# Five expert pairs' outputs written to DRAM rows and gathered back per token, in a decoder layer with a mixture of experts

## The chip, the cores and the metric

The kernel runs on one core of one Trainium2 chip. The metric is device time in microseconds of one execution; the kernel before takes 704.09 us (median of three runs, 701.79 to 704.62). Its engines are named as in the profile: PE is TensorE, DVE is VectorE, ACT is ScalarE, POOL is GpSimd and SP is SyncE, which issues most DMAs.

## The reference

One decoder layer over 512 tokens of width 1024: two attention branches, then a mixture of 32 experts, then a norm. The change touches the mixture alone. In float32:

```python
def hierarchical_moe(h, w_rg, b_rg, w_re, b_re, w_g, w_u, w_d):
    ...
    g_sel = jnp.argmax(g_logits, axis=-1).astype(jnp.int32)
    ...
    top_vals, top_idx = lax.top_k(e_in, EXPERT_TOPK)
    weight = p_group * jax.nn.softmax(top_vals, axis=-1)
    expert_id = g_sel[:, None] * EXPERTS_PER_GROUP + top_idx.astype(jnp.int32)
    ...
    def expert_block(args):
        xb, e = args
        return (jax.nn.silu(xb @ w_g[e]) * (xb @ w_u[e])) @ w_d[e]
    ...
    out = jnp.zeros((T, D), h.dtype).at[slot_tok].add(ys * slot_w[:, None])
```

Each token chooses one of four groups and two of its eight experts. It is computed by these two, and their outputs, weighted, are added to its row. An expert has three matrices of 1 MB: gate and up (1024 x 256) and down (256 x 1024).

## The kernel before

The attention part runs to about 396 us, the output projection with the routing to about 435 us, and the experts from there to the end. The last two parts matter here.

**Routing.** For each of the four tiles of 128 tokens, DVE finds the group and the two experts (`choose_group`, `choose_experts`), PE counts the places of the tokens within their experts (`ranks`), and DVE turns these into one-hot matrices (`hot`, `AB`) with which PE finds the token of each slot and the first pair's rows. The tile `Mk` holds the two one-hot rows of a token's experts, `n` its two places. These operations are written in Python in this order, but the framework's scheduler sets the order on DVE, ACT and SP. Only PE's and POOL's order within the expert loop (and DVE's and ACT's in the last pair) is that of the code.

**Experts.** They are taken in 16 pairs; of a pair's 128 slots the first 64 belong to one expert and the rest to the other. The loop in `experts` does for pair q:

- SP issues the six loads of 1 MB for pair q+2 (`load_gu`, `load_d`). They go in turn through a ring of 20 buffers (`new_w`, `NH = 20`), and `load` lets each wait for the load two before it, so that two are under way.
- PE multiplies the gathered, transposed rows `xT` by gate (G) and up (U), 32 matmuls each (L770); ACT and DVE make `a = silu(G) * U` (L775, L776), PE transposes it (L782), ACT copies it back as `aT` (L784).
- PE makes the products `yp` with down in two halves of 512 columns (L796). `down_split` scales each by the slots' weights and splits it into a rounded part and a remainder: ACT L803, DVE L804.
- The combines put the slots' rows back to their tokens. `one_hot` makes S (slots by 512 tokens); for each half and each tile of tokens, PE multiplies S by the two parts (L816, L817) and DVE adds the result to `x2`, the residual in SBUF (L818). The eight combines of pair q are done in pair q+1, five behind U and three behind the transposes of a, where they fill PE's wait for a.
- POOL gathers the rows (`xg`) and the weights (`wg`) of pair q+2 from DRAM by an indirect DMA that skips empty slots (L729), and copies the slots' weights into a small tile `sw` (L739, L740).

In the last pair `last` adds the final norm: ACT scales the norm's gain `fin` (L882), which SP loads among the last weights, and the tiles of tokens are squared, scaled and stored.

```python
    def load(self, dst, src):
        d = self.nc.sync.dma_start(dst, src)
        if len(self.loads) >= 2:
            self.after(d, self.loads[-2])
```

Of the kernel before, what the change touches and what calls it, by code (L numbers as in the profile page):

```python
# [10 lines left out]
F32 = mybir.dt.float32  # L11
# [3 lines left out]
I32 = mybir.dt.int32  # L15
U32 = mybir.dt.uint32
AF = mybir.ActivationFunctionType
ALU = mybir.AluOpType
# [3 lines left out]
P = 128  # L22
T = 512
NT = T // P
D = 1024
# [5 lines left out]
NEG = -1e30  # L31
NE = 32
NH = 20


class Layer:
# [84 lines left out]
    def setup(self):  # L121
        nc, tc, ctx, io = self.nc, self.tc, self.ctx, self.io
        self.const = ctx.enter_context(tc.tile_pool(name="const", bufs=1, side="left"))
        self.small = ctx.enter_context(tc.tile_pool(name="small", bufs=1, side="left"))
        self.big = ctx.enter_context(tc.tile_pool(name="big", bufs=16, side="left"))
        c = self.const
        self.ident = c.tile([P, P], F32, name="ident")
        make_identity(nc, self.ident)
        self.mhalf = c.tile([P, 1], F32, name="mhalf")
        nc.gpsimd.memset(self.mhalf, -0.5)  # L130
        self.eps = c.tile([P, 1], F32, name="eps")
        c.tile([P, 24], F32, name="pad")
        nc.gpsimd.memset(self.eps, EPS * D)

    def load_consts(self):
# [472 lines left out]
    def take_weights(self):  # L608

        nc = self.nc  # L610
        ps = self.mp.tile([P, 512], F32, name="ptr", tag="m")[:, 0:NE + 1]
        for t in range(NT):
            nc.tensor.matmul(ps, self.hot[:, t], self.W[:, t], start=t == 0, stop=t == NT - 1)
        return self.slot_weights(0, ps, nc.vector)

    def clean_rows(self):

# [13 lines left out]
    def route_setup(self):  # L631
        nc, tc, io, c = self.nc, self.tc, self.io, self.const
        self.dram = dp = self.ctx.enter_context(tc.tile_pool(name="dram", bufs=1, space=bass.MemoryType.DRAM))
        self.x2d = dp.tile([T, D], F32, name="x2d")
        self.Wd = dp.tile([T, NE + 1], F32, name="Wd")
        self.wr = c.tile([P, KD, 40], F32, name="wr")
        nc.gpsimd.memset(self.wr, 0.0)
        self.load_late(self.wr[:, :, 0:4], io["w_router_group"][0].rearrange("(j p) g -> p j g", p=P))
        for g in range(4):
            self.load_late(self.wr[:, :, 8 + 8 * g:16 + 8 * g],  # L640
                              io["w_router_expert"][0, g].rearrange("(j p) e -> p j e", p=P))
        self.gpj = c.tile([P, KD], F32, name="gpj")
        self.load_late(self.gpj, io["ffn_norm"][0].rearrange("(p j) -> p j", p=P))
        self.gcol = gcol = c.tile([P, KD], F32, name="gcol")
        self.load_late(gcol, io["ffn_norm"][0].rearrange("(j p) -> p j", p=P))
        nc.vector.tensor_scalar(self.gpj, self.gpj, 32.0, None, ALU.mult)
        nc.vector.tensor_scalar(gcol, gcol, 32.0, None, ALU.mult)
        nc.vector.tensor_tensor(self.wr, self.wr, gcol.unsqueeze(2).to_broadcast([P, KD, 40]), ALU.mult)
        self.rb = c.tile([P, 40], F32, name="rb")
        nc.gpsimd.memset(self.rb, -3e38)  # L650
        self.load_late(self.rb[:, 0:4], io["b_router_group"][0:1, :].to_broadcast([P, 4]))
        self.load_late(self.rb[:, 8:40], io["b_router_expert"].rearrange("o g e -> o (g e)")
                          .to_broadcast([P, 32]))
        self.rc = c.tile([P, 33 + NT], F32, name="rc")
        self.load_late(self.rc, io["rconst"])
        self.iota32 = self.rc[:, 0:32]
        self.slot = self.rc[:, 32:33]
        self.token = self.rc[:, 33:33 + NT]
        self.tri = c.tile([P, 2, P], F16, name="tri")
        self.after(nc.gpsimd.dma_start(self.tri, io["tri"]), self.started)  # L660
        self.tm = c.tile([P, T], F16, name="tm")
        self.after(nc.gpsimd.dma_start(self.tm, io["tm"]), self.started)
        self.M = c.tile([P, NT, NE], F16, name="M")
        self.sq = c.tile([P, 2, NT], F32, name="sq")
        self.W = c.tile([P, NT, NE + 1], F32, name="W")
        self.iotaU = c.tile([P, NE], U32, name="iotaU")
        nc.vector.tensor_copy(self.iotaU, self.iota32)
# [10 lines left out]

    def load(self, dst, src):
        d = self.nc.sync.dma_start(dst, src)  # L680
        if len(self.loads) >= 2:
            self.after(d, self.loads[-2])
        self.loads.append(d)

    def load_w(self, src, how):
# [45 lines left out]
                                         bounds_check=T - 1, oob_is_err=False)  # L731
        return xg, wg

    def slot_weights(self, q, wg, eng):

        sw = self.small.tile([P, 2], F32, name="sw", tag="sw", bufs=3)
        for e in range(2):
            es = slice(64 * e, 64 * e + 64)
            eng.tensor_copy(sw[es, 0:1], wg[es, 2 * q + e:2 * q + e + 1])  # L739
        eng.tensor_copy(sw[:, 1:2], wg[:, NE:NE + 1])  # L740
        return sw[:, 0:1], sw[:, 1:2]

    def gathered_T(self, xg, xT, g):
        nc = self.nc
# [34 lines left out]
    def act_T(self, a, ps):  # L779
        nc = self.nc  # L780
        for j in range(2):
            nc.tensor.transpose(ps[:, j * P:(j + 1) * P], a[:, j * P:(j + 1) * P], self.ident)  # L782
        aT = a.rearrange("p (a b) -> p a b", b=P)
        nc.scalar.copy(aT, ps.rearrange("p (a b) -> p a b", b=P))  # L784
        return aT

    def down(self, wd, aT, sw, half):
# [24 lines left out]
    def combine(self, S, y, half, t):  # L812
# [4 lines left out]
        nc.tensor.matmul(cp, S[:, t * P:(t + 1) * P], y[1], start=False, stop=True)  # L817
        nc.vector.tensor_tensor(self.x2[t][:, hs], self.x2[t][:, hs], cp, ALU.add)  # L818

    def experts(self):  # L820
        nc, tc = self.nc, self.tc
        NP = NE // 2
# [3 lines left out]
        self.yhl = self.wp.tile([P, 2048], F32R, name="yhl", tag="whi")  # L826
        with tc.manual_schedule(engines={mybir.EngineType.PE, mybir.EngineType.Pool}):
            xT, sw, xg = {0: self.xT0}, {}, {}
            S, y, todo = None, None, []
            for q in range(NP):  # L830
                if q > 0 and q + 2 < NP:
                    wgu[q + 2], wd[q + 2] = self.load_gu(q + 2), self.load_d(q + 2)
                    if q + 2 == NP - 1:
                        self.load_final()
                if q:
                    sw[q] = self.slot_weights(q, wg, nc.gpsimd)

                def some(n):
                    for _ in range(min(n, len(todo))):
                        self.combine(S, y[todo[0][0]], *todo[0])  # L840
                        todo.pop(0)

                def between(j):
                    if q == 0 and j == 3:
                        self.tokens()
                        xg[1] = self.gather_rows(self.xi[:, 1:2], self.rows)
                    if q == 0 and j == 5:
                        sw[0] = self.take_weights()
                    if q == 0 and j == 9:
                        self.count_blocks()  # L850
                a = self.gate_up(wgu.pop(q), xT.pop(q), lambda: sw[q][1], between)
                def next_rows():
                    xT[q + 1] = self.new_xT()
                    for g in range(2):
                        self.gathered_T(xg[q + 1][0], xT[q + 1], g)
                if q == 0:
                    next_rows()
                some(5)
                aT = self.act_T(*a)
                some(3)  # L860
                if 0 < q < NP - 1:
                    next_rows()
                if q + 1 < NP:
                    wg = xg.pop(q + 1)[1]
                if q + 2 < NP:
                    xg[q + 2] = self.gather_rows(self.xi[:, q + 2:q + 3])
                S = self.one_hot(self.xf[:, q:q + 1])
                dn = wd.pop(q)
                y = [None, None]
                todo = [(h, t) for h in range(2) for t in range(NT)]  # L870
                if q == NP - 1:
                    self.last(S, dn, aT, sw[q][0])
                    break
                for h in range(2):
                    y[h] = self.down(dn, aT, sw[q][0], h)
# [159 lines left out]
class Route:  # L1035
# [60 lines left out]
    def choose_experts(self):  # L1096
# [1 line left out]
        self.v8, vi = self.tmp("v8", [8]), self.tmp("vi", [8], U32)  # L1098
        nc.vector.max(self.v8, self.es)
        nc.vector.max_index(vi, self.v8, self.es)  # L1100
        self.Mk = self.tmp("Mk", [2, NE])
        nc.vector.tensor_tensor(self.Mk, L.iotaU.unsqueeze(1).to_broadcast([P, 2, NE]),
                                vi[:, 0:2].unsqueeze(2).to_broadcast([P, 2, NE]), ALU.is_equal)
        nc.vector.tensor_tensor(L.M[:, self.t], self.Mk[:, 0], self.Mk[:, 1], ALU.add)
# [15 lines left out]

    def places(self):
        nc, L, t, N = self.nc, self.L, self.t, self.N
        n = self.tmp("n", [2])
        for c in range(2):
            nc.vector.scalar_tensor_tensor(self.es, self.Mk[:, c], 1.0, N, ALU.mult, ALU.mult, accum_out=n[:, c:c + 1])
        self.at(self.AB[:, :, 0:64], n)
# [33 lines left out]
def shape_consts():  # L1160
# [13 lines left out]
    tri[:, 0] = np.arange(P)[:, None] <= np.arange(P)[None, :]  # L1174
    tri[:, 0] += 1024.0 * np.eye(P)
    out["tri"] = tri
    rc = np.zeros((P, 33 + NT), np.float32)
    rc[:, 0:32] = np.arange(32)
    rc[:, 32] = 1025 + np.arange(P) % 64
    rc[:, 33:] = np.arange(P)[:, None] + P * np.arange(NT)[None, :] - 1024  # L1180
    out["rconst"] = rc
    out["tm"] = np.broadcast_to(np.arange(T, dtype=np.float32) - 1024, (P, T)).copy()
    return out
# [30 lines left out]
```

## Time and profile before

| what | us |
|---|---|
| median of the runs | 704.09 |
| the profiled execution | 708.18 |
| its span in the profile | 706.4 |
| PE busy | 684.0 (97%) |
| DVE busy | 399.0 (56%) |
| ACT busy | 277.3 (39%) |
| POOL busy | 70.9 (10%) |
| HBM read, written | 145.35 MB, 4.26 MB |

The profile is of one execution, whose time stands beside its span. The page's second part cuts the span into 40 slices and gives for each the busy tenths of an engine, of the granted TensorE clock and of the 16 DMA engines, and the GB/s that they moved. In a row of a group of instructions stand its line, engine and operation, output<-input, the count, then the busy time and the mean of one in ns, and the idle time before them with what ended it. SP's rows are issues of DMAs, and their times hold no transfer.

### The profile page before, as it was taken

The numbers are of one execution on the slowest core, as the hardware profiler recorded it, in microseconds if no ns is written. First come the engines' busy times: TensorE is split into PE (matmuls) and PEld (weight loads), VectorE is DVE, ScalarE is ACT, GpSimd is POOL, SyncE is SP. The second block draws the span as 40 slices with busy tenths as digits, with TensorE's granted clock in tenths as the row PEclk, the third lists the DMA queues.
The fourth block names the chain that finished last, engine by engine and source line by source line (L and its number), as shares of the span: only waits on it lengthen the run. The fifth ranks groups of instructions, "written<-read, shape, count | busy, mean of one in ns | idle before, by whom it ended". The sixth has DMA issues, their size and how long they took to land.

```text
span 706.4 us, 11377 instructions
## 1 busy us (share of the span) xinstructions
PE 684.0 (97%) x4262; PEld 526.2 (74%) x4262; DVE 399.0 (56%) x972; ACT 277.3 (39%) x623; POOL 70.9 (10%) x151
## 2 busy tenths in 40 slices
PE   8999999999999999999999999999999999999981
PEld 7998887777888888888888998665666666656641
DVE  4535957877829963433764227355554455555545
ACT  5748554555648663431332433121211211222113
POOL 1504000000000000000000013112111111121003
PEclk9999999999999999999999999999999999999997
DMA  8734431110272143213889668989999999999833
GB/s 253 137 77 84 111 120 60 60 45 17 69 170 61 44 138 119 63 57 119 269 295 370 243 220 296 401 309 365 367 344 347 364 357 379 374 354 370 319 123 121
DMA packets 73787, 148.17 MB, mean 210 GB/s; under 512 B 30939, under 2 KB 53555, under 8 KB 61953
## 3 DMA queue, kind: packets, MB, share of 16 engines
q1 hardware_dynamic: 67616, 138.69, 56.2%
q10 hardware_dynamic: 3040, 4.27, 2.3%
q0 software_dynamic: 3072, 4.46, 2.2%
q8 instruction: 35, 0.57, 0.3%
q14 instruction: 24, 0.19, 0.1%
HBM read 145.35 MB, written 4.26 MB: 212 GB/s over the span
## 4 chain that ended last, share of the span: by engine, by line
PE 90%; DMA 4%; DVE 2%; ACT 2%; issue 1%; SPq 0%; POOL 0%; POOLq 0%; ACTq 0%; DVEq 0%
PE yp L796 8%; PE G L770 7%; PE U L770 7%; PE pacc L96 5%; PE pacc L95 5%; PE pacc L94 5%; PE pacc L450 4%; PE pacc L448 4%; PE pacc L449 4%; PE cp L816 4%; PE cp L817 3%; PE ptr L421 3%; PE S L403 2%; PE O L429 2%; PE pacc L492 2%; PE pacc L494 2%
## 5 line engine op out<-in xcount | busy, mean ns | idle before, releaser
L65 DVE SCALAR_TENSOR_TENSOR wlo<-wraw,ms,whi 128x256 fp32r<-128x256 f32 (+2 forms) x134 | 68.3, 551 | 30.6 <-ACT whi L64 30.4
L64 ACT ACTIVATE whi<-wraw,ms 128x256 fp32r<-128x256 f32 (+2 forms) x134 | 67.0, 560 | 41.6 <-PE pacc L449 19.8
L818 DVE TENSOR_TENSOR x<-x,cp 128x512 f32<-128x512 f32 x128 | 78.1, 681 | 1.8 <-PE cp L817 1.8
L94 PE MATMUL pacc<-whi,hThi 128*128 128x352 f32 (+1 forms) x192 | 72.8, 379 | 0.0
L95 PE MATMUL pacc<-wlo,hThi 128*128 128x352 f32 (+1 forms) x192 | 70.2, 367 | 0.0
L96 PE MATMUL pacc<-whi,hTlo 128*128 128x352 f32 (+1 forms) x192 | 70.2, 366 | 0.0
L796 PE MATMUL yp<-w,a 128*64 128x512 f32 x256 | 60.2, 613 | 3.3 <-ACT a L784 3.3
L776 DVE SCALAR_TENSOR_TENSOR a<-U,sw,a 128x256 f32<-128x256 f32 x16 | 11.0, 687 | 84.2 <-PE U L770 78.6
L770 PE MATMUL U<-w,xT 128*64 128x256 f32 x512 | 58.5, 379 | 0.0
L770 PE MATMUL G<-w,xT 128*64 128x256 f32 x512 | 58.3, 380 | 0.0
L770 PEld LDWEIGHTS G<-w,xT 128*64 128x64 f32 x512 | 36.5, 137 | 24.6 <-issue 4.9
L816 PE MATMUL cp<-yhl,S 128*128 128x512 f32 x128 | 53.2, 416 | 0.0
L817 PE MATMUL cp<-yhl,S 128*128 128x512 f32 x128 | 50.6, 395 | 0.7 <-DVE yhl L804 0.7
L770 PEld LDWEIGHTS U<-w,xT 128*64 128x64 f32 x512 | 37.8, 137 | 17.6
L448 PE MATMUL pacc<-hThi,whi 128*128 128x512 f32 x128 | 50.4, 394 | 0.0
L450 PE MATMUL pacc<-hThi,wlo 128*128 128x512 f32 x128 | 50.3, 393 | 0.0
L449 PE MATMUL pacc<-hTlo,whi 128*128 128x512 f32 x128 | 49.9, 390 | 0.0
L804 DVE SCALAR_TENSOR_TENSOR yhl<-yp,sw,yhl 128x512 fp32r<-128x512 f32 x32 | 24.0, 751 | 34.9 <-ACT yhl L803 33.9
L416 ACT ACTIVATE E<-E,mx 128x128 f32<-128x128 f32 (+3 forms) x64 | 35.6, 558 | 20.4 <-DVE mx L413 19.6
L796 PEld LDWEIGHTS yp<-w,a 128*64 128x64 f32 x256 | 17.3, 139 | 34.3 <-issue 28.7
L803 ACT ACTIVATE yhl<-yp,sw 128x512 fp32r<-128x512 f32 x32 | 22.0, 687 | 48.3 <-PE yp L796 46.3
L94 PEld LDWEIGHTS pacc<-whi,hThi 128*128 128x128 f32 x192 | 36.4, 189 | 4.9 <-issue 1.4
(221 smaller groups left out, 1328.8 us busy)
## 6 DMA issues: line engine op xcount, KB each, us to landing
w<-in_w_exp_gate_dram SPq DMA_DIRECT2D x32, 1024.0 KB, 6.3
w<-in_w_exp_up_dram SPq DMA_DIRECT2D x32, 1024.0 KB, 6.9
w<-in_w_exp_down_dram SPq DMA_DIRECT2D x30, 1024.0 KB, 5.7
wraw<-in_w_in_dram SPq DMA_DIRECT2D x14, 1024.0 KB, 5.1
wraw<-in_w_out_dram SPq DMA_DIRECT2D x4, 1024.0 KB, 8.2
wraw<-in_w_in_dram SPq DMA_DIRECT2D x5, 704.0 KB
xs<-in_x_dram SPq DMA_DIRECT2D x4, 512.0 KB, 7.8
wraw<-in_w_o_mla_dram SPq DMA_DIRECT2D x4, 512.0 KB, 4.7
```

Source lines behind the costliest of these rows:

```text
L65: nc.vector.scalar_tensor_tensor(lo[:, k], raw[:, k], g, hi[:, k].bitcast(F32), ALU.mult, ALU.subtract)
L94: nc.tensor.matmul(ps[t][:, :ncols], act_hi[kk // 4][:, kk % 4, ts], hi[:, k], start=kk == 0, stop=False)
L95: nc.tensor.matmul(ps[t][:, :ncols], act_hi[kk // 4][:, kk % 4, ts], lo[:, k], start=False, stop=False)
L96: nc.tensor.matmul(ps[t][:, :ncols], act_lo[kk // 4][:, kk % 4, ts], hi[:, k], start=False, stop=kk == ktot - 1)
L448: nc.tensor.matmul(ps, hi[:, k, ds], self.hT[0][k // 4][:, k % 4], start=k == 0, stop=False)
L449: nc.tensor.matmul(ps, hi[:, k, ds], self.hT[1][k // 4][:, k % 4], start=False, stop=False)
L450: nc.tensor.matmul(ps, lo[:, k, ds], self.hT[0][k // 4][:, k % 4], start=False, stop=k == KD - 1)
L770: nc.tensor.matmul(GU[i][es, 0:256], xT[:, j, es], gu[e][i][:, j * 256:(j + 1) * 256], start=j == 0, stop=j == KD - 1)
L796: nc.tensor.matmul(yp[es], aT[:, j, es], wd[e][:, j * D + half * 512:j * D + half * 512 + 512], start=j == 0, stop=j == 1)
L816: nc.tensor.matmul(cp, S[:, t * P:(t + 1) * P], y[0], start=True, stop=False)
L817: nc.tensor.matmul(cp, S[:, t * P:(t + 1) * P], y[1], start=False, stop=True)
L818: nc.vector.tensor_tensor(self.x2[t][:, hs], self.x2[t][:, hs], cp, ALU.add)
```

## The change

Pairs 1, 3, 5, 7 and 9 (`VIA`) are combined in another way. Their outputs are scaled by ACT into a tile `y` of 128 slots, which POOL stores into a DRAM tensor `yd` of 5 x 128 rows (`down_out`). They have no S, no split and no combines. In pairs 10 to 13, one tile of tokens in each, POOL clears two tiles and gathers into them the rows that belong to each token's first and second expert, with an index out of bounds where that expert isn't in one of the five pairs (`take_slots`). DVE adds the two tiles to `x2` one pair later. `slot_rows` works out the row indices from `Mk` and the places, which are now kept in SBUF for all four tiles.

Further, the eight combines of the other pairs up to 8 are spread over the two pairs that follow, four in each. The slots' weights are copied by ACT behind the copy of `aT`, and the scale of silu and up is read directly from `wg`, so POOL copies nothing in the loop. `load` lets three loads be under way.

```diff
+VIA = (1, 3, 5, 7, 9)
...
     def load(self, dst, src):
         d = self.nc.sync.dma_start(dst, src)
-        if len(self.loads) >= 2:
-            self.after(d, self.loads[-2])
+        if len(self.loads) >= 3:
+            self.after(d, self.loads[-3])
...
-    def slot_weights(self, q, wg, eng):
+    def slot_weights(self, q, wg, copy):
         sw = self.small.tile([P, 2], F32, name="sw", tag="sw", bufs=3)
         for e in range(2):
             es = slice(64 * e, 64 * e + 64)
-            eng.tensor_copy(sw[es, 0:1], wg[es, 2 * q + e:2 * q + e + 1])
-        eng.tensor_copy(sw[:, 1:2], wg[:, NE:NE + 1])
-        return sw[:, 0:1], sw[:, 1:2]
+            c = copy(sw[es, 0:1], wg[es, 2 * q + e:2 * q + e + 1])
+            if q:
+                self.after(c, self.acted)
+        return sw
...
+    def slot_rows(self):
...
+        for t in range(NT):
+            for i in range(2):
+                nc.vector.scalar_tensor_tensor(junk, self.Mk[:, t, i], 1.0, self.base, ALU.mult, ALU.mult,
+                                               accum_out=rows[:, t, i:i + 1])
+        nc.vector.tensor_scalar(far, self.place, 1088.5, float(1 << 20), ALU.is_gt, ALU.mult)
+        nc.vector.tensor_tensor(rows, rows, self.place, ALU.add)
+        self.yi = c.tile([P, NT, 2], I32, name="yi")
+        nc.vector.tensor_tensor(self.yi, rows, far, ALU.add)
+
+    def down_out(self, wd, aT, sw, q):
+        nc = self.nc
+        y = self.bl.tile([P, D], F32, name="y", tag="yd", bufs=2)
+        for h in range(2):
+            nc.scalar.mul(y[:, h * 512:h * 512 + 512], self.down_products(wd, aT, h), sw)
+        i = VIA.index(q) * P
+        nc.gpsimd.dma_start(self.yd[i:i + P], y)
+
+    def take_slots(self, t, i):
+        nc = self.nc
+        y = self.bl.tile([P, D], F32, name="y", tag="yd", bufs=2)
+        nc.gpsimd.memset(y, 0.0)
+        nc.gpsimd.indirect_dma_start(out=y, out_offset=None, in_=self.yd,
+                                     in_offset=bass.IndirectOffsetOnAxis(ap=self.yi[:, t, i:i + 1], axis=0),
+                                     bounds_check=len(VIA) * P - 1, oob_is_err=False)
+        return t, y
...
-                if q:
-                    sw[q] = self.slot_weights(q, wg, nc.gpsimd)
+                r = wg[:, NE:NE + 1] if q else None
...
-                a = self.gate_up(wgu.pop(q), xT.pop(q), lambda: sw[q][1], between)
+                a = self.gate_up(wgu.pop(q), xT.pop(q), lambda: r if q else sw[0][1], between)
...
-                some(5)
+                n = min(len(todo), 4) if VIA[0] <= q <= VIA[-1] + 1 else len(todo)
+                some((n + 1) // 2 + (n > 4))
                 aT = self.act_T(*a)
-                some(3)
+                if q:
+                    sw[q] = [self.slot_weights(q, wg, nc.scalar.copy)[:, 0:1]]
+                some(n // 2 - (n > 4))
...
                     xg[q + 2] = self.gather_rows(self.xi[:, q + 2:q + 3])
+                if q == 1:
+                    self.slot_rows()
+                for t, r in taken:
+                    nc.vector.tensor_tensor(self.x2[t], self.x2[t], r, ALU.add)
+                t = q - VIA[-1] - 1
+                taken = [self.take_slots(t, i) for i in range(2)] if 0 <= t < NT else []
+                dn = wd.pop(q)
+                if q in VIA:
+                    self.down_out(dn, aT, sw[q][0], q)
+                    continue
                 S = self.one_hot(self.xf[:, q:q + 1])
```

What moves, at three places. First PE in pair 2, from U to the products with down, before (buffer numbers left out; U is the up product, cp a combine, G with `ident` the transposes of a, ptr those of the next rows):

```order
L770 MATMUL U<-w,xT 64x256 x16
...
L816 MATMUL cp<-yhl,S 128x512
L817 MATMUL cp<-yhl,S 128x512
L782 MATMUL G<-ident,a 128x128 x2
L816 MATMUL cp<-yhl,S 128x512
L817 MATMUL cp<-yhl,S 128x512
...
L747 MATMUL ptr<-ident,xg 128x128 x8
L796 MATMUL yp<-w,a 64x512 x8
```

Left out are four more pairs of cp rows ahead of the transposes and two more behind. The same place now:

```order
L778 MATMUL U<-w,xT 64x256 x16
L824 MATMUL cp<-yhl,S 128x512
L825 MATMUL cp<-yhl,S 128x512
...
L790 MATMUL G<-ident,a 128x128 x2
L824 MATMUL cp<-yhl,S 128x512
L825 MATMUL cp<-yhl,S 128x512
...
L755 MATMUL ptr<-ident,xg 128x128 x8
L804 MATMUL yp<-w,a 64x512 x8
```

One more pair of cp rows is left out on either side: of eight combines four are left, two ahead of the transposes and two behind, and so in each of pairs 1 to 10.

Second, DVE in the routing, where the second tile's experts have just been chosen (M), before (es,n gives a place, AB and hot are the one-hot matrices, f and W the routing weights):

```order
L1104 TENSOR_TENSOR M<-Mk 128x32
L1125 SCALAR_TENSOR_TENSOR es,n<-Mk,ptr 128x32 x2
L1118 SCALAR_TENSOR_TENSOR AB<-tm,n 128x2x64
L1152 SCALAR_TENSOR_TENSOR f<-f 128x1
```

and now:

```order
L1157 TENSOR_TENSOR M<-Mk 128x32
L1178 SCALAR_TENSOR_TENSOR es,place<-Mk,ptr 128x32
L836 SCALAR_TENSOR_TENSOR yjunk,yrows<-Mk,rc 128x32
L1178 SCALAR_TENSOR_TENSOR es,place<-Mk,ptr 128x32
L836 SCALAR_TENSOR_TENSOR yjunk,yrows<-Mk,rc 128x32
L1171 SCALAR_TENSOR_TENSOR AB<-tm,place 128x2x64
L1205 SCALAR_TENSOR_TENSOR f<-f 128x1
```

The operations of `slot_rows`, written in pair 1, stand among the routing, two for each tile of tokens; for tiles 1 and 2 (of 0 to 3) they stand among the place operations that AB waits for, and `hot` follows behind.

Third, ACT at the end of the loop, before (a<-G with sw is silu, COPY a<-G the copy of `aT`):

```order
L754 ACTIVATE xT<-ptr,gpj 128x128 x2
L803 ACTIVATE yhl<-yp,sw 128x512 x2
L775 ACTIVATE a<-G,sw 128x128x2
L882 ACTIVATE fin<-fin 128x1024
L784 COPY a<-G 128x256
```

and now:

```order
L811 ACTIVATE yhl<-yp,sw 128x512 x2
L783 ACTIVATE a<-G,wg 128x128x2
L792 COPY a<-G 128x256
L746 COPY sw<-wg 64x1 x2
L935 ACTIVATE fin<-fin 128x1024
```

The scale of `fin` stood ahead of the last pair's copy and stands behind it now, with the two copies of weights between.

More of the change, by code (lines that the diff above doesn't have):

```diff
@@ L131, in setup @@
         self.eps = c.tile([P, 1], F32, name="eps")
-        c.tile([P, 24], F32, name="pad")
+        c.tile([P, 16], F32, name="pad")
         nc.gpsimd.memset(self.eps, EPS * D)
@@ L613, in take_weights @@
             nc.tensor.matmul(ps, self.hot[:, t], self.W[:, t], start=t == 0, stop=t == NT - 1)
-        return self.slot_weights(0, ps, nc.vector)
+        sw = self.slot_weights(0, ps, nc.vector.tensor_copy)
+        nc.vector.tensor_copy(sw[:, 1:2], ps[:, NE:NE + 1])
+        return sw[:, 0:1], sw[:, 1:2]
     def clean_rows(self):
@@ L634, in route_setup @@
         self.x2d = dp.tile([T, D], F32, name="x2d")
+        self.yd = dp.tile([len(VIA) * P, D], F32, name="yd")
         self.Wd = dp.tile([T, NE + 1], F32, name="Wd")
@@ L653, in route_setup @@
                           .to_broadcast([P, 32]))
-        self.rc = c.tile([P, 33 + NT], F32, name="rc")
+        self.rc = c.tile([P, 33 + NT + NE], F32, name="rc")
         self.load_late(self.rc, io["rconst"])
@@ L658, in route_setup @@
         self.token = self.rc[:, 33:33 + NT]
+        self.base = self.rc[:, 33 + NT:]
         self.tri = c.tile([P, 2, P], F16, name="tri")
@@ L663, in route_setup @@
         self.M = c.tile([P, NT, NE], F16, name="M")
+        self.Mk = c.tile([P, NT, 2, NE], F32, name="Mk")
+        self.place = c.tile([P, NT, 2], F32, name="place")
         self.sq = c.tile([P, 2, NT], F32, name="sq")
@@ L783, in act_T @@
         aT = a.rearrange("p (a b) -> p a b", b=P)
-        nc.scalar.copy(aT, ps.rearrange("p (a b) -> p a b", b=P))
+        self.acted = nc.scalar.copy(aT, ps.rearrange("p (a b) -> p a b", b=P))
         return aT
@@ L818, in combine @@
         nc.vector.tensor_tensor(self.x2[t][:, hs], self.x2[t][:, hs], cp, ALU.add)
+    def slot_rows(self):
+        nc, c = self.nc, self.const
+        rows = c.tile([P, NT, 2], F32, name="yrows")
+        far = c.tile([P, NT, 2], F32, name="far")
+        junk = c.tile([P, NE], F32, name="yjunk")
+        for t in range(NT):
[21 more added lines that the diff above has]
+        return t, y
     def experts(self):
@@ L828, in experts @@
             xT, sw, xg = {0: self.xT0}, {}, {}
-            S, y, todo = None, None, []
+            S, y, todo, taken = None, None, [], []
             for q in range(NP):
@@ L866, in experts @@
                     xg[q + 2] = self.gather_rows(self.xi[:, q + 2:q + 3])
+                if q == 1:
[8 more added lines that the diff above has]
+                    continue
                 S = self.one_hot(self.xf[:, q:q + 1])
-                dn = wd.pop(q)
                 y = [None, None]
@@ L1100, in choose_experts @@
         nc.vector.max_index(vi, self.v8, self.es)
-        self.Mk = self.tmp("Mk", [2, NE])
+        self.Mk = L.Mk[:, self.t]
         nc.vector.tensor_tensor(self.Mk, L.iotaU.unsqueeze(1).to_broadcast([P, 2, NE]),
@@ L1122, in places @@
         nc, L, t, N = self.nc, self.L, self.t, self.N
-        n = self.tmp("n", [2])
+        n = L.place[:, t]
         for c in range(2):
@@ L1176, in shape_consts @@
     out["tri"] = tri
-    rc = np.zeros((P, 33 + NT), np.float32)
+    rc = np.zeros((P, 33 + NT + NE), np.float32)
     rc[:, 0:32] = np.arange(32)
     rc[:, 32] = 1025 + np.arange(P) % 64
-    rc[:, 33:] = np.arange(P)[:, None] + P * np.arange(NT)[None, :] - 1024
+    rc[:, 33 + NT:] = [64 * (2 * VIA.index(i // 2) + i % 2) - 1025 if i // 2 in VIA else 1 << 20 for i in range(NE)]
+    rc[:, 33:33 + NT] = np.arange(P)[:, None] + P * np.arange(NT)[None, :] - 1024
     out["rconst"] = rc
```

## The prediction

> **What bounds the kernel now.** I read the page's slices first, then the end of the chain of work, then SP's waits, then windows over the weight stream.
>
> ```profile
> span 706.4 us, 11377 instructions
> PE   8999999999999999999999999999999999999981
> DMA  8734431110272143213889668989999999999833
> GB/s 253 137 77 84 111 120 60 60 45 17 69 170 61 44 138 119 63 57 119 269 295 370 243 220 296 401 309 365 367 344 347 364 357 379 374 354 370 319 123 121
> ```
>
> One slice is 17.7 us. PE is busy nearly everywhere, which suggests a kernel bound by TensorE. But from slice 26 on (about 442 us) the DMA engines are at nine tenths too. Two resources are full at once, so the end of the chain has to decide.
>
> ```profile
> 636.76 3.45 PE G L770 x32
> ...
> 643.67 0.43 PE cp L816
> ...
> 646.18 0.22 PE G L782 x2
> ...
> 647.56 0.24 PE cp L817
> ...
> 648.81 3.58 PE yp L796 x16
> 652.39 3.45 PE G L770 x32
> 655.85 3.45 PE U L770 x32
> ...
> 659.81 7.13 DMA w<-in_w_exp_up_dram
> ...
> 667.00 5.80 DMA w<-in_w_exp_down_dram
> ...
> 673.42 7.27 DMA fin<-in_final_norm_dram
> ...
> 680.76 0.04 ACT fin L882
> 680.80 0.92 issue
> 681.72 0.36 ACT a L784
> ...
> 682.13 5.35 PE yp L796 x16
> ```
>
> Each row is a start, a length and what ran. A pair of experts takes PE 652.39 - 636.76 = 15.6 us, up to pair 14. Then the chain leaves PE: the last weights, issued one after another from 659.8 us, are what the last pair waits for. PE and the weight stream thus arrive together, the stream a little later. SP's waits between 450 and 676 us tell what paces the stream (total us, times, longest):
>
> ```profile
> SPq L680 <- DMA w<-in_w_exp_gate_dram: 66.3, 24, 4.2
> SPq L680 <- DMA w<-in_w_exp_up_dram: 65.9, 23, 4.5
> SPq L680 <- DMA w<-in_w_exp_down_dram: 63.8, 26, 4.0
> SPq L680 <- PE cp L817: 2.3, 9, 0.4
> SPq L680 <- PE yp L796: 1.7, 6, 0.4
> ```
>
> 196 of the 226 us SP waits for an earlier load (the limit of two under way), and about 4 us for PE to free a buffer. So the stream runs by itself and not at PE's pace. How fast it is (last three columns: granted clock, DMA share, GB/s):
>
> ```profile
> 450.00:460.00 10.00, 10.00 (x76) 7.01 (x73) 4.51 (x8) 1.09 (x2) 0.37 (x2) 1.00 1.00 397
> 566.00:567.50 1.50, 1.50 (x8) 1.24 (x7) 1.50 (x4) 0.00 (x0) 0.00 (x0) 1.00 1.00 426
> 594.50:596.20 1.70, 1.70 (x20) 1.12 (x18) 0.00 (x0) 0.43 (x1) 0.37 (x2) 1.00 0.55 145
> 450.00:650.00 200.00, 200.00 (x1360) 126.09 (x1358) 105.98 (x180) 38.76 (x76) 32.59 (x63) 1.00 0.96 359
> 450.00:676.00 226.00, 226.00 (x1544) 142.91 (x1541) 117.00 (x199) 43.94 (x85) 34.76 (x70) 1.00 0.94 351
> ```
>
> 426 GB/s while every engine has packets, 397 over the best 10 us, 351 on the average. Between lie holes such as 594.5 to 596.2 us, where half of the engines have nothing: both loads under way are nearly through, and the next has only just been issued. That is the loss which a third load can fill.
>
> **The change part by part.**
>
> *PE.* Five pairs lose their eight combines of two matmuls. In the chain above the 16 matmuls go from 643.67 to 647.80 us with 0.22 us of transposes among them: 3.9 us, 16 x 0.24. Five pairs: 18.8 us less PE work (bounds 17 to 19.5; the four combines left in each of pairs 1 to 10 keep the cover, two ahead of the transposes of a and two behind, 0.9 us each). This is worth time only as far as the weights come earlier, because PE already meets them at the end.
>
> *New traffic.* Five stores of 512 KB are 2.62 MB. The gathers fetch what five of sixteen pairs hold: on the average 5/16 of 512 x 2 slots, 320 rows of 4 KB, 1.31 MB. All of it runs on the engines that carry the weights.
>
> ```profile
> q0 software_dynamic: 2306, 3.66, 5.2%
> ```
>
> That is POOL's queue from 450 to 676 us: 3.66 MB took 5.2% of 226 us, 11.8 us or 3.2 us for a MB. By it the new 3.93 MB cost 12.6 us; by their bytes at 351 GB/s, 11.2 us; at 426, 9.2 us.
>
> *Three under way.* No run here has it, so it is bounded: from below by nothing (351 stays), from above by no hole and no slow restart at all (397 over 10 us; 426 only over 1.5 us). Taking the holes out alone gives 351 / 0.94 = 373; restarts after a hole are slow as well, and they go with it. I take **385**, the middle of 373 and 397. Before: 351 x 226 us = 79.3 MB. After: 83.2 MB at 385 = 216.1 us, **-9.9 us**. At 397: 209.6, -16.4. At 373: 223.1, -2.9. At 359: 231.8, +5.8. The break-even is 83.2 / 226 = 368 GB/s. The start hardly moves: the load issued at 450 us needs a buffer that pair 0's products free at 449 us.
>
> *The routing stage.* Eight multiplies with a sum and three small operations are written in pair 1, but the order shows them on DVE among the routing, where DVE is in the chain:
>
> ```profile
> 425.88 0.42 DVE x L497
> ...
> 428.53 0.21 DVE es L1125 x2
> ...
> 430.12 0.21 DVE hot L1118
> 430.37 1.16 PE pacc L604 x8
> ```
>
> ```profile
> L1125 DVE SCALAR_TENSOR_TENSOR es<-Mk,ptr 128x32 f32<-128x32 f32 x8 | 1.5, 183 | 0.1
> L1125 DVE DVE_READ_ACCUMULATOR es<-Mk,ptr 128x1 f32 x8 | 0.7, 81 | 0.0
> ```
>
> The like operation costs 183 + 81 ns, with some overlap 0.2 us. Four stand in DVE's way to the last but one `hot` (two for tile 1, two for tile 2); the rest falls into waits for PE, or behind it. **+0.8 us** (bounds 0 to 2.6).
>
> *The tail.* Today ACT scales `fin` ahead of the last copy of a, so the copy at 681.72 us waits for a transfer that it doesn't need. In the new order the copy stands ahead. The second half of the last products still needs the last down weights, issued at 675.7 us. **-1.2 us** (bounds -2.5 to +1: after the stop before 682.13 us the 16 products took 5.35 us, where they took 3.58 at 648.81; a PE that waits for weights earlier in the last pair can lose such 1.8 us there too).
>
> *At nothing.* The weights' copies on ACT instead of POOL (two of a column), the products' scaling (one ACT operation where there were ACT and DVE), POOL's memsets and the eight adds on DVE:
>
> ```profile
> L60 DVE TENSOR_TENSOR wlo<-wraw,whi 128x1024 fp32r<-128x1024 f32 x8 | 9.5, 1221 | 7.9 <-ACT whi L59 7.9
> L620 POOL MEMSET xg<- 128x1024 f32 x1 | 0.9, 947 | 0.0
> xg<-x2d,xi POOLq DMA_INDIRECT x13, 7.4
> ```
>
> Two adds put 2.4 us on DVE between the scaled rows and the split of y, which is next needed after G and U, 6.9 us on; DVE is busy 117 of 226 us. The adds wait for a gather issued a pair earlier: it lands in about 7 us, a pair has 11 or more. If it landed after 15 us, DVE would stand, and behind it the split, a and the combines; only then would it cost. POOL's store waits for ACT's second half of y; behind it stands nothing until the next pair's row gather, which waits for PE anyway.
>
> Sum: -9.9 + 0.8 - 1.2 = **-10.3 us**. The profiled execution took 708.18 us with a span of 706.4, 4.1 us over the median, so about 697.9 for a profiled one and **693.8** for the median of 704.09.
>
> **The rivals.**
>
> *Bytes decide.* The third load adds no rate: the engines share what the memory gives, and 359 GB/s over 200 us is that. Then the new 3.93 MB are paid, and PE waits the longer. Place: weights of the last pairs; it decides below 368 GB/s. At 359: +5.8 + 0.8 - 1.2 = +5.4, **709.5**; at 351 it would be 715. For it: 200 us of an even 359 at a share of 0.96. Against it: 397 over 10 us and 426 beside a hole of 145.
>
> The Trainium skill has this as a rule: "DMA: Bandwidth & Descriptors", section "Where 436 GB/s comes from", says that for transfers between HBM and SBUF the HBM side binds, at about 358 GB/s for a core; by it the time would be 710 us. The window of 397 GB/s speaks against it in a run on one core, and "HBM Reference", section "Specifications (TRN2)", itself grants a core that streams alone more.
>
> *PE decides.* If the stream goes above about 400 GB/s, PE's own 18.8 us are the limit: -18.8 + 0.8 - 1.2 = -19.2, **684.9**. For it: 426 while no engine is empty. Against it: gathers and stores come in bursts, and the best 10 us have 397.
>
> *The third load doesn't get in.* It needs a free buffer as well as the limit; were buffers the limit, SP would wait for PE, and the time would be that of 351 GB/s, **715**. PE rows of 4 us against 196 speak against it, and PE gets faster, so buffers come earlier.
>
> *A tie.* Rates of 366 to 375 GB/s give +0.9 to -4.5 us: nothing to tell, 700 to 705.
>
> **How the numbers follow.** Forecast (375 to 400 GB/s) 0.58; PE decides 0.08; tie 0.14; bytes decide 0.17; no third load 0.03. A difference under 0.5%, 3.5 us, can't be told from none. Faster by more: 0.67; within: 0.14; slower: 0.19. The range goes from PE's limit to the bytes' rival, 685 to 709.5; beyond lie some 6% below and 10% above. The forecast's own range is 688 to 700.
>
> **What would show it.** Right: the window from 450 us to the last up weights at 375 GB/s or more with a share of 0.97 and above; hardly any hole of half-empty engines; gate loads of successive pairs 16 to 17.5 us apart; PE with waits for weights in the last three or four pairs, where it had none; the copy of a ahead of `fin`. Wrong: a window rate under 368 (bytes), SP waiting for PE (buffers), PE without a wait to the end (PE decides). DVE's `hot` later by under 0.3 or over 1.5 us would refute the routing term. The prediction fails altogether if DVE waits for the gathered rows in pairs 11 to 14.

## The result and the profile after

The changed kernel takes **683.64 us** (median of four runs, 682.90 to 684.24); the kernel before took 704.36 us on the same chip (701.79 to 708.88). The ratio is 0.971, 95% interval 0.968 to 0.975. The gain of 20.7 us is twice the forecast of 10.3, and the time lies 1.4 us below the range. The case that came true is the rival "PE decides", to which the prediction gave a chance of 0.08 and for which it had worked out 684.9.

The page of the changed kernel, its span, PE's slices and the DMA rows (a slice is now 17.0 us):

```profile
span 681.9 us, 11080 instructions
...
PE   7999999999999999999999999999999999999991
...
DMA  7733442101073026221398948799999999999953
GB/s 254 128 103 66 86 163 73 62 1 62 15 200 96 1 63 185 68 87 62 137 331 306 392 169 287 256 408 408 409 415 416 410 410 414 415 412 416 413 194 125
```

From slice 26 to slice 37 (counted from 0) the GB/s row is flat at 408 to 416, where it went up and down between 309 and 379 before. Windows over the same stretch of the changed kernel (last three columns: granted clock, DMA share, GB/s):

```profile
450.00:460.00 10.00, 10.00 (x78) 6.66 (x76) 4.48 (x8) 2.09 (x6) 0.54 (x1) 1.00 1.00 407
450.00:650.00 200.00, 200.00 (x1414) 122.47 (x1412) 92.66 (x150) 48.62 (x112) 47.18 (x47) 1.00 1.01 412
```

The 200 us window has 412 GB/s against 359 before, and no less than its own first 10 us. Finer still, the DMA view of that window in 40 slices of 5 us, first of the kernel before:

```profile
GB/s 418 377 253 294 370 370 368 349 362 368 289 413 419 315 326 346 347 367 309 381 270 400 416 338 393 337 378 401 373 344 403 370 346 393 352 360 338 375 359 374
```

and of the changed kernel:

```profile
GB/s 414 400 415 399 420 402 409 411 393 419 424 417 416 421 409 422 410 421 393 378 424 417 420 421 415 406 426 412 416 412 403 413 418 418 405 420 416 408 412 405
```

Before, single slices reach 413 to 419 and others fall to 253; after, nearly all stand at the height of the best ones before. With the stream that fast, PE meets no weights that are late. All of PE's waits in the changed kernel from 400 us to the end (us in total, times, longest):

```profile
PE cp L825 <- DVE yhl L812: 0.7, 1, 0.7
PE yp L804 <- ACT a L792: 0.5, 1, 0.5
```

and the end of its chain of work:

```profile
445.45 3.65 PE yp L804 x16
...
568.52 3.58 PE yp L804 x16
...
582.19 3.58 PE yp L804 x16
...
597.82 3.58 PE yp L804 x16
...
644.72 3.58 PE yp L804 x16
...
659.34 3.58 PE yp L804 x16
```

The chain stays on PE up to the last products, with no DMA in it. A pair with four combines takes 582.19 - 568.52 = 13.67 us, one with eight 597.82 - 582.19 = 15.63 us, as before. The difference between the two profiles' spans, 706.4 - 681.9 = 24.5 us, can therefore be read off step by step, to 0.1 us:

| part | us |
|---|---|
| first yp (445.35 before) | +0.1 |
| ten pairs, from the first yp to the eleventh: 136.74 instead of 156.56 | -19.8 |
| PE's wait before the last yp, gone: 2.8 of it was for ACT's copy of `a`, which stood behind the load of `fin` (33.32 between the last two yp before, 15.63 + 14.62 without a wait) | -3.1 |
| last yp: 3.58 at a granted clock of 1.00 instead of 5.35 at 0.68 | -1.8 |

### The profile page after: what moved, and what is told of

Same layout as the page of the kernel before. It is cut to its first block, busy times and chain, and to the rows that moved or that the text cites. A ratio compares the mean times of both kernels' runs of the same rounds, so it can differ in the third digit from the quotient of the medians.

```text
span 681.9 us, 11080 instructions
## 1 busy us (share of the span) xinstructions
PE 661.3 (97%) x4182; PEld 508.6 (75%) x4182; DVE 376.1 (55%) x944; ACT 283.3 (42%) x653; POOL 83.3 (12%) x127
## 4 chain that ended last, share of the span: by engine, by line
PE 92%; DVE 4%; ACT 1%; DMA 1%; issue 1%; POOL 0%; SPq 0%; POOLq 0%; DVEq 0%
PE yp L804 8%; PE G L778 8%; PE U L778 8%; PE pacc L97 5%; PE pacc L96 5%; PE pacc L95 5%; PE pacc L451 4%; PE pacc L449 4%; PE pacc L450 4%; PE cp L824 3%; PE ptr L422 3%; PE cp L825 3%; PE S L404 3%; PE O L430 2%; PE pacc L493 2%; PE pacc L494 2%
## 5 line engine op out<-in xcount | busy, mean ns | idle before, releaser
L65 ACT ACTIVATE whi<-wraw,ms 128x256 fp32r<-128x256 f32 (+2 forms) x134 | 67.0, 560 | 42.1 <-PE pacc L450 19.8
L784 DVE SCALAR_TENSOR_TENSOR a<-U,wg,a 128x256 f32<-128x256 f32 x15 | 10.3, 686 | 101.8 <-issue 68.9
L804 PE MATMUL yp<-w,a 128*64 128x512 f32 x256 | 58.5, 598 | 0.5 <-ACT a L792 0.5
L826 DVE TENSOR_TENSOR x<-x,cp 128x512 f32<-128x512 f32 x88 | 54.2, 682 | 0.8 <-PE cp L825 0.8
L96 PEld LDWEIGHTS pacc<-wlo,hThi 128*128 128x128 f32 x192 | 36.6, 191 | 4.2 <-issue 0.7
L804 PEld LDWEIGHTS yp<-w,a 128*64 128x64 f32 x256 | 17.0, 136 | 30.2 <-issue 27.8
L97 PEld LDWEIGHTS pacc<-whi,hTlo 128*128 128x128 f32 x192 | 36.4, 189 | 3.9 <-issue 0.2
L824 PE MATMUL cp<-yhl,S 128*128 128x512 f32 x88 | 37.6, 427 | 0.0
```

Source lines behind the costliest of these rows:

```text
L65: nc.scalar.mul(hi[:, k], raw[:, k], g)
L96: nc.tensor.matmul(ps[t][:, :ncols], act_hi[kk // 4][:, kk % 4, ts], lo[:, k], start=False, stop=False)
L97: nc.tensor.matmul(ps[t][:, :ncols], act_lo[kk // 4][:, kk % 4, ts], hi[:, k], start=False, stop=kk == ktot - 1)
L804: nc.tensor.matmul(yp[es], aT[:, j, es], wd[e][:, j * D + half * 512:j * D + half * 512 + 512], start=j == 0, stop=j == 1)
L824: nc.tensor.matmul(cp, S[:, t * P:(t + 1) * P], y[0], start=True, stop=False)
```

## The experiments

Each was timed beside the kernel before on the same chip. With the first four experiments below it took 703.98 us (13 runs), with the one that puts POOL's copies ahead of the gathers 702.25 (7 runs), with the other four 703.25 (17 runs).

### The third load without the rest

```diff
     def load(self, dst, src):
         d = self.nc.sync.dma_start(dst, src)
-        if len(self.loads) >= 2:
-            self.after(d, self.loads[-2])
+        if len(self.loads) >= 3:
+            self.after(d, self.loads[-3])
         self.loads.append(d)
```

> The kernel before with one line changed: three loads may be under way instead of two. Theory A (the third load fills the holes, whatever else is in the kernel): the window from 450 to 650 us shows 400 GB/s or more at a share of 0.99 or more, where before it showed 359 at 0.96; PE then has no wait in the last pair, and the time falls only by those waits (2.8 us ahead of the last products, and some 1.8 us for their slow start in the profile): 700 to 703 us. Theory B (the rate rose because five pairs load DVE, PSUM and the queues less, not because of the third load): the window stays at 350 to 365 GB/s and the time at 704.

Measured: 705.31 us, ratio 1.001 (0.998 to 1.004), so no gain. Its window and, of the waits between 450 and 650 us, those of the routing weights:

```profile
450.00:650.00 200.00, 199.50 (x1352) 124.51 (x1348) 103.81 (x177) 38.21 (x75) 31.77 (x62) 1.00 1.00 404
```

```profile
POOL sw L739 <- DMA wg<-Wd,xi: 84.4, 13, 7.6
...
ACT a L775 <- POOL sw L740: 62.7, 12, 5.8
DVE a L776 <- ACT a L775: 40.0, 7, 6.5
```

The same three waits in the kernel before, over the same stretch:

```profile
POOL sw L739 <- DMA wg<-Wd,xi: 67.7, 13, 6.8
...
ACT a L775 <- POOL sw L740: 48.3, 11, 5.7
...
DVE a L776 <- ACT a L775: 5.6, 1, 5.6
```

The stream did what theory A said: 404 GB/s instead of 359. The time did not follow. A weight gather lands later beside a fuller stream, so POOL's copy is later, so the silu on ACT, and the product on DVE now waits for the silu in seven pairs. In one of them PE stands; here is the chain:

```profile
508.55 3.58 PE yp L796 x16
...
519.48 0.73 ACT a L775
...
520.76 0.69 DVE x L818
...
525.19 3.58 PE yp L796 x16
```

That pair takes 525.19 - 508.55 = 16.64 us instead of 15.63. The kernel is bound by PE now, and PE still has all 256 combine matmuls to do. Theory A's 700 to 703 was therefore too low: it was right on the stream and wrong on what the time would make of it. Theory B's 704 is nearer the time, but its 350 to 365 GB/s is refuted.

### Two loads under way in the changed kernel

```diff
-        if len(self.loads) >= 3:
-            self.after(d, self.loads[-3])
+        if len(self.loads) >= 2:
+            self.after(d, self.loads[-2])
```

> The changed kernel with two loads under way as before; all else of the change stays. Theory A: the stream falls back to 351 to 365 GB/s, carries 83.2 MB instead of 79.3, and the last pairs wait for their weights: 83.2 / 0.358 = 232 us from 450 us to the last up weights, some 29 us more than with three, of which PE's 18.8 us less work can't hide any: 706 to 716 us, so slower than the kernel before. Theory B: 684 us and a window of 400 GB/s or more.

Measured: 729.50 us, ratio 1.032 (1.025 to 1.040): slower than before by 25 us. Its window, and PE's waits from 450 to 697 us:

```profile
450.00:650.00 200.00, 180.72 (x1215) 107.47 (x1212) 71.92 (x118) 42.17 (x97) 40.27 (x41) 0.97 0.94 342
```

```profile
PE U L778 <- DMA w<-in_w_exp_up_dram: 25.4, 9, 4.8
PE G L778 <- DMA w<-in_w_exp_gate_dram: 2.4, 3, 1.7
```

PE waits 27.8 us for weights. The direction is that of theory A, but its size was too small by 13.5 to 23.5 us: with two loads under way the engines move even less than before (342 against 359 GB/s), and the granted clock falls to 0.97 in this window. That the new stores and gathers lower the rate is likely, but no run shows it alone. Five pairs less PE work are worth nothing at that rate; they cost time.

### Four loads under way

```diff
-        if len(self.loads) >= 3:
-            self.after(d, self.loads[-3])
+        if len(self.loads) >= 4:
+            self.after(d, self.loads[-4])
```

> The changed kernel with four loads under way. Theory A: the engines are already never empty with three (share 1.01, 412 GB/s), so nothing is left to fill: 412 GB/s, 683 to 685 us. Rival: the rate still rises with each load under way; then the window shows over 420 GB/s, and the time stays at 683 to 684 all the same, because PE has no waits.

Measured: 682.55 us, ratio 0.970 (0.968 to 0.972), within about 1 us of the changed kernel and 0.45 us under theory A's range. Its window:

```profile
450.00:650.00 200.00, 200.00 (x1416) 122.43 (x1414) 92.11 (x149) 48.55 (x112) 47.09 (x47) 1.00 1.01 414
```

A fourth load adds 2 GB/s, so theory A holds. From the first yp to the last this run takes 213.8 us, as the changed kernel does; its first yp only came earlier, at 444.05 against 445.45 us. The fourth load shows in the landing times instead.

### Four pairs instead of five

```diff
-VIA = (1, 3, 5, 7, 9)
+VIA = (1, 3, 5, 7)
```

> The changed kernel with four pairs through DRAM rows (1, 3, 5, 7) instead of five; their rows are gathered in pairs 8 to 11. If PE's own work decides with the stream at 412 GB/s: 16 more matmuls of 0.244 us, +3.9 us, 687.5. If the stream still decides (its last weights land at 659.9 us, when PE begins the last products at 659.3): 0.79 MB less at 412 GB/s, -1.9 us, 681.7.

Measured: 686.16 us, ratio 0.975 (0.973 to 0.977), 2.5 us more than the changed kernel. Pair 9's combines are 3.9 us of PE; the first yp of this run comes 1.35 us earlier (444.10 against 445.45 us), which leaves 2.55. PE decides: had the stream been the limit, the 0.8 MB less would have made it no slower.

### Third load and copies on ACT, all combines kept

```diff
+                r = wg[:, NE:NE + 1] if q else None
-                if q:
-                    sw[q] = self.slot_weights(q, wg, nc.gpsimd)
...
                 aT = self.act_T(*a)
+                if q:
+                    sw[q] = [self.slot_weights(q, wg, nc.scalar.copy)[:, 0:1]]
```

> The kernel before with two parts of the change: three loads under way, and the routing weights no longer copied by POOL (the activation reads the gathered row, ScalarE copies the slot weights behind the aT copy). All five pairs are still combined by matmul, so nothing leaves the computation. Theory A (in three_only the late gathers held POOL's copies, these the silu, this the product on DVE and TensorE; the pairs between 476 and 620 us took up to 16.64 instead of 15.63 us): pairs of 15.6 us again in that stretch, no DVE wait for ScalarE's a (40.0 us there), the last yp near 679 and 700 to 702.5 us. Rival B (the longer pairs come from a TensorE that reads its operands or is clocked less well under the denser stream): the pairs stay at 15.7 to 16.6 us and the time at 704.5 to 706.

The edit of `load` is that of the run with the third load alone; the silu reads `r`.

Measured: 702.75 us (701.54 to 703.53, ten runs), ratio 0.998 (0.996 to 1.001). Its chain, and all that ACT's silu waits for:

```profile
475.16 3.58 PE yp L799 x16
...
490.79 3.58 PE yp L799 x16
```

```profile
ACT a L778 <- PE G L773: 36.0, 13, 2.8
```

Every pair takes 15.63 us again, and the silu waits for PE alone. Theory A holds: the long pairs of the run with the third load alone came from POOL's copies. The time stands 0.25 us above what A gave, because PE's own 16 pairs take that long whether weights come early or not. The last yp starts at 677.38 us, the first at 443.81: 233.57 us, against 659.34 - 445.45 = 213.89 in the changed kernel. The difference is 19.7 us, the ten shorter pairs and nothing else.

### Copies on POOL, all else changed

```diff
-                r = wg[:, NE:NE + 1] if q else None
+                if q:
+                    sw[q] = [self.slot_weights(q, wg, nc.gpsimd.tensor_copy)]
+                    nc.gpsimd.tensor_copy(sw[q][0][:, 1:2], wg[:, NE:NE + 1])
+                    sw[q] = sw[q][0][:, 0:1], sw[q][0][:, 1:2]
...
-                if q:
-                    sw[q] = [self.slot_weights(q, wg, nc.scalar.copy)[:, 0:1]]
```

> The changed kernel with all routing weights copied by POOL again at the head of each pair, as before, and the silu reading the copy. Theory A (the edit that the prediction took at nothing is worth time once three loads are under way, since POOL's copies stand behind the next gather): stalls as in three_only, of which the pairs are shorter here (13.7 us) so that a late gather hurts more: 686 to 692 us, with ScalarE's silu waiting for POOL. Rival B (the taken edit is free, the output gathers are not in its way): 683 to 684.5 us.

Left out are the silu, which reads the copy again, and the order of the copies behind the copy of `aT`, which is gone.

Measured: 708.82 us, ratio 1.007 (1.004 to 1.010). The part that the prediction took at nothing is worth 25 us, far beyond theory A's 686 to 692. Two windows:

```profile
450.00:560.00 110.00, 110.00 (x794) 66.44 (x792) 41.02 (x69) 24.67 (x48) 23.11 (x44) 1.00 1.01 411
...
580.00:600.00 20.00, 14.72 (x103) 8.89 (x102) 5.39 (x10) 3.07 (x6) 6.53 (x9) 0.98 1.02 418
```

Up to 560 us PE is busy all the time, and the stream runs at 411 GB/s: the loss is not there. It begins where the output gathers do, with pair 10. POOL between pairs 10 and 11, in time:

```profile
582.46 1.05 POOL L736 DMA_INDIRECT xg<-x2d,xi  x1 [4.61 <-PE ptr L753]
583.81 1.00 POOL L736 DMA_INDIRECT wg<-Wd,xi  x1 [0.30 <-issue]
...
588.28 1.00 POOL L855 DMA_INDIRECT y<-yd,yi  x1 [0.27 <-POOL y L854]
589.28 0.19 POOL L746 COPY sw<-wg 64x1 f32<-64x1 f32 x1
598.61 0.18 POOL L746 COPY sw<-wg 64x1 f32<-64x1 f32 x1 [9.14 <-DMA y<-yd,yi]
```

The first copy runs at once, so the pair's weights are long there. The second waits 9 us for the output gather that was issued just ahead of it. The program's order on POOL shows why (the DMASW names are counters of POOL's own DMAs; `sw` reads a `wg` that was fetched a pair earlier):

```
L736 DMA xg<-x2d,xi 128x1024 [waits PE_49]
L736 DMA wg<-Wd,xi 128x33 [waits Pool_49]
L854 MEMSET y 128x1024 [waits DMASW0_49]
L855 DMA y<-yd,yi 128x1024 [waits DMASW5_49,Pool_49]
L854 MEMSET y 128x1024
L855 DMA y<-yd,yi 128x1024 [waits Pool_49]
L746 COPY sw<-wg 64x1 [waits DVE_49]
L746 COPY sw<-wg 64x1 [waits DMASW6_49,DMASW7_49,DMASW1_49,DMASW0_49]
```

The second copy carries waits on four counters, one for each gather above it. In pairs without output gathers it has two. The waits from 560 to 690 us show who inherits it:

```profile
ACT a L781 <- POOL sw L877: 52.8, 6, 12.5
...
PE cp L822 <- DVE x L824: 18.2, 3, 6.4
```

The silu waits for POOL, the product on DVE for the silu, and the combines on PE for the adds behind that product. PE stands 18.2 us in all, and from 600 to 660 us, where it works for 47.1 us, its granted clock is 0.83 to 0.85; that costs some 7.7 us more, an estimate from these numbers. Together this is about the 25 us.

### The same copies on POOL, ahead of the gathers

```diff
                     wg = xg.pop(q + 1)[1]
+                    p = self.slot_weights(q + 1, wg, nc.gpsimd.tensor_copy)
+                    nc.gpsimd.tensor_copy(p[:, 1:2], wg[:, NE:NE + 1])
+                    sw[q + 1] = p[:, 0:1], p[:, 1:2]
                 if q + 2 < NP:
                     xg[q + 2] = self.gather_rows(self.xi[:, q + 2:q + 3])
```

The lines that made the copies at the head of the pair are gone.

> The kernel of pool_copies with POOL's three copies for a pair moved ahead of the gathers for the pair after it, a pair earlier. Nothing is left out; there are as many copies on POOL, of the same tiles. Theory A (POOL copies cost 25 us in pool_copies because the second copy of a pair carries a wait for the two gathers issued just ahead of it, output gathers among them): with the copies ahead of these gathers the wait is for gathers issued a pair earlier, 13.7 us or more, which land in 8 to 10: no wait of the silu for POOL, pairs of 13.7 and 15.6 us, 683 to 685 us. Rival B (POOL copying at all while the output gathers run is what costs, or the memsets of 1 us ahead of them): 690 us or more.

Measured: 683.18 us, ratio 0.972 (0.969 to 0.975), level with the changed kernel. The waits from 450 to 650 us:

```profile
POOL sw L746 <- DMA wg<-Wd,xi: 66.7, 14, 7.3
...
ACT a L781 <- PE G L776: 39.9, 14, 3.1
...
POOL sw L746 <- DMA y<-yd,yi: 22.7, 4, 6.0
```

POOL waits for gathers as long as ever, the output gathers included, but a pair ahead of the silu, which waits for PE alone. So it was the place of the copies in POOL's queue that cost 25 us, and neither POOL's copying nor its memsets.

### Six pairs, with three loads and with four

```diff
-VIA = (1, 3, 5, 7, 9)
+VIA = (1, 3, 5, 7, 8, 9)
```

> The changed kernel with a sixth pair (8) through DRAM rows, three loads under way. Pairs 9 and 10 then have no combine to lie between the gate and up products and the aT copy. Theory A (TensorE's path decides and the stream has nothing left): TensorE loses 16 x 0.244 = 3.9 us of matmuls, gives back 1 to 2 us for each of the two uncovered pairs, and the stream has 0.8 MB more, some 1.9 us at 412 GB/s, with the last weights landing at 660 to 662 us against a last yp that would come at 657.5: 683 to 686 us, and TensorE waits for weights in the last pairs. Rival B (the stream still has room): 680 to 682 us and no such wait.

> Six pairs through DRAM rows and four loads under way. Theory A (at 414 GB/s the stream is as full as it gets): within 1.5 us of via_six, 682 to 685, since a fourth load only starts the stream a little earlier. Rival B (via_six is held by holes in the stream): 679 to 681.

The second run also has the edit of `load` of the run with four loads.

Measured: 683.47 us (ratio 0.970, 0.966 to 0.974) and, with four loads, 683.36 us (0.971, 0.968 to 0.975). The chain with three loads:

```profile
580.16 3.58 PE yp L804 x16
...
593.08 7.88 DMA w<-in_w_exp_up_dram
...
659.65 3.58 PE yp L804 x16
```

At 580.16 us PE is 2.0 us ahead of the changed kernel (582.19): the 3.9 us, less the 1.7 that it waits for `a` in the two pairs without combines. Then, from 593.08 to 635.83 us, the chain goes through weight loads, PE waits 0.8 us for one, and the last yp starts at 659.65, not earlier than the changed kernel's 659.34. The stream is the next limit, and it is reached: theory A, in both runs. No version beat the changed kernel by more than the 1 us of the one with four loads.

## Why the prediction was wrong

**What bounds the kernel before.** Right. PE and the stream arrived together, and both had to gain: the third load alone gives 705.3 us, the five pairs on two loads 729.5, both together 683.6. Neither part is worth anything by itself.

**PE, -18.8.** Right in kind, small by 1.0: ten pairs lose 19.8 us in all. The prediction's own 3.9 us for each of five pairs make 19.5; why it took 18.8 it does not say. Four combines kept in each pair are cover enough: the only wait for `aT` in the whole stage, 0.5 us, is that of pair 0.

**Three under way, 385 GB/s.** This is the step that failed: the mechanism was right and the size was not. The prediction took the middle of 373 and 397; it was 412. At 412 the 83.2 MB take 202 us instead of 226, which is 24 us less and more than PE's 18.8, so the sum should have been made on PE. PE decides above 83.2 / (226 - 18.8) = 402 GB/s. The upper bound was the weak point. "No hole and no slow restart at all" was put at 397, "over the best 10 us". But 450 to 460 us are not the best 10 us: of the 5 us slices of the same trace two neighbours, 505 to 515 us, hold 413 and 419, and the window over both has 416. (Nor is 359 over 200 us "even": the slices go from 253 to 419.) Taking the middle of the bounds was the other part of the error: between 373 and 416 it is 394.5, still -15.1, while the upper bound itself gives -26 and so PE. With no hole left, the rate was that of the best stretches. How much of the rise is from holes and how much from faster packets isn't settled: the share alone, 0.94 to 1.01, gives 377.

**Bytes decide.** Wrong: in this run on one core 412 GB/s stood for 200 us. The Trainium skill's rule ("DMA: Bandwidth & Descriptors", section "Where 436 GB/s comes from") that the HBM side binds at about 358 GB/s would have given 710 us. The Trainium skill's "HBM Reference", section "Specifications (TRN2)", has about 425 for a core that streams alone. The traces come near that and stay under it: 414 with four loads, 415 with six pairs and four loads.

**PE decides.** Right in mechanism, and the near number is in part luck. Its terms add up to -19.2 us, while the two profiles differ by 24.5: PE gave 1.0 more, the routing cost 0.7 less, the tail gave 3.7 more. The profiled execution of before was also 4.1 us over the median from which 684.9 was counted.

**No third load.** Wrong, as forecast: from 450 to 650 us SP waits 171.6 us for loads and 5.2 for PE.

**The routing stage, +0.8.** It is +0.1. DVE in the changed kernel, at the second tile:

```profile
428.42 0.18 DVE L1178 SCALAR_TENSOR_TENSOR es<-Mk,ptr 128x32 f32<-128x32 f32 x1
...
428.52 0.19 DVE L836 SCALAR_TENSOR_TENSOR yjunk<-Mk,rc 128x32 f32<-128x32 f32 x1
...
428.64 0.19 DVE L1178 SCALAR_TENSOR_TENSOR es<-Mk,ptr 128x32 f32<-128x32 f32 x1
```

and in the kernel before:

```profile
428.30 0.18 DVE L1125 SCALAR_TENSOR_TENSOR es<-Mk,ptr 128x32 f32<-128x32 f32 x1
...
428.53 0.19 DVE L1125 SCALAR_TENSOR_TENSOR es<-Mk,ptr 128x32 f32<-128x32 f32 x1
```

The two `es` operations start 0.23 us apart before and 0.22 after, with the new one between them. The last but one `hot` starts at 430.15 us where it started at 430.04, later by 0.1: under 0.3, which the prediction had named as what would refute this term. The new operations went into gaps that DVE had anyway; a mean duration does not show such gaps, the starts do.

**The tail, -1.2.** It is -4.9: 3.1 us of wait and 1.8 us of slow clock. Both the new order of ACT and the earlier weights can have a share, and no run separates them. In the changed kernel the copy of `a` runs at 657.98 us and the scaling of `fin` at 659.69, after the last products have begun at 659.34; behind `fin` the copy would have come too late for them. The run with the third load alone doesn't have the old order either: there the scheduler, by the edit of `load` alone, puts the copy (679.65 us) ahead of `fin` (679.92).

**From the profile to the median.** The prediction took 4.1 us off, since the profiled execution of before was that much over the median. The steps add up to -24.5 us between the profiles and the medians differ by 20.7: the profiled execution of before had 4.9 us of waits and slow clock at its end. Whether its other executions had less of them no trace shows. With PE as the bound the profile is as fast as the median (683.7 against 683.64).

**At nothing: the copies on ACT.** The adds, the memsets and the scaling on ACT cost nothing, as said; DVE never waits for a gathered row. The copies' move is not nothing. Without it, or a place ahead of the gathers, the kernel takes 708.8 us. The trace of before held the warning: the silu waited 48.3 us for POOL there, up to 5.7 at a time, under cover of U and five combines. The prediction asked what ACT's copies would cost, not what POOL's would have cost with two more gathers in the same queue.

**What would show it.** Gate loads of successive pairs are issued 16.9 us apart (449.13 to 634.81 us in eleven steps), the share is 1.01 and the rate over 375: right. PE was to wait for weights in its last pairs: wrong, and named as the sign for "PE decides".

## What to carry to other kernels

Where two resources reach the end together, price each of them alone at its best rate and take the slower; the best rate is read from the best of many short windows, not from one, and where the change takes away what makes the holes, that rate and not a middle is the forecast. When gathers are added to a queue, look at which small operation behind them carries a wait for them and who waits for that: a copy of 0.18 us cost 25 us by its place. A part that is worth nothing alone may be what lets the others count.

## What the runs showed of the hardware

The landing times of loads, by the number under way, from the pages' rows on gate loads (last number: us from issue to landing), of the kernel before, of the one with three loads and copies on ACT, and of the one with four loads:

```profile
w<-in_w_exp_gate_dram SPq DMA_DIRECT2D x32, 1024.0 KB, 6.3
```

```profile
w<-in_w_exp_gate_dram SPq DMA_DIRECT2D x32, 1024.0 KB, 8.0
```

```profile
w<-in_w_exp_gate_dram SPq DMA_DIRECT2D x32, 1024.0 KB, 10.6
```

Loads under way by their size over the landing time give 2 x 1.05 MB / 6.3 us = 333 GB/s, 3 x 1.05 / 8.0 = 393 and 4 x 1.05 / 10.6 = 396. The windows from 450 to 650 us of these runs have 359, 400 and 414 GB/s. The third load buys rate, the fourth mostly waits longer. The other side of it: what shares the engines lands later too, such as the gathers of weights that POOL waited for: 6.1 us from 445 to 650 us in the kernel before, 7.8 in the run with the third load alone.
